# Moving VectorE's and ScalarE's side work, a check's small matmuls and the last block's transfers in a TensorE-bound two-layer kernel

## The chip, the cores and the metric

One core of one Trainium2 chip. The metric is the device time of a launch in microseconds (us), slowest core, median of runs; executions of one kernel mostly agree within 0.3%. A trace of one execution goes with it; its span is about 1.5 us shorter than the time.

## The reference

```python
batch, m, k, h, n = 16, 512, 768, 3072, 768        # x: (16, 512, 768)
y = np.maximum(np.matmul(x, w1) + b1, 0)
return np.matmul(y, w2).astype(np.float32)
```

## The kernel before

The 8192 rows are worked off in 16 blocks: 8 blocks of rows with the first half of the hidden units, then the same rows with the second half, whose results are added to the outputs that the first eight blocks wrote. Both products run in fp16 in a seven-product (Strassen-like) or 20-product form, so that TensorE does fewer matmuls and the other engines form sums of inputs, weights and results. The 20 products of the second layer are the 20 "steps" of a block; this table names what follows each (engine, where to, from which pair of PSUM banks):

```python
SECOND = (
    ("mm", 16, 1, True), ("mm", 4, 0, True), ("ACT", "s0", 1, 1), ...
    # ... steps 2 to 6
    ("mm", 11, 1, False),  ("DVE", "o2", 1, -1, "s4", 1),      # step 7: o2 = s4 - q1
    ("mm", 3, 0, False),   ("ACT", "s5", 0, 1),                # step 8
    ("mm", 8, 2, True),    ("ACT", "q1", 2, 1),                # step 9: banks q2 into banks q1
    ("mm", 1, 0, False),   ("DVE", "o3", 0, -1, "s0", 1),      # step 10
    ("mm", 13, 2, False),  ...                                 # step 11: adds into q2 again
    # ... steps 12 to 18
    ("mm", 7, 3, False),   ("DVE", "o6", 3, -1, "s4", 1),      # step 19
)
```

Steps and their products are counted from 0: in the texts below "product 11" is the product of step 11, written `("mm", 13, ...)`, which reads the weights' sum V13. V6, V14 and B5 are other blocks or sums of w2; the negated B5 is formed on ScalarE. VectorE's and ScalarE's work runs in the order in which the program emits it (the prediction shows it in a trace). Extra work (sums of weights and of x, squares for the range check, loads) is hooked behind a step by `put(kind, block, group, step, what)`; `"m1"` is a group of the first product, `"m2"` the second product:

```python
for n in range(15):                                   # sums of w2, two halves each, first block
    put("p1", 0, *divmod(min(10 + n // 2, 15), 4), self.sum_w2, n, 0, 2)
    late = {9: 1, 7: 2, 8: 3, 12: 4, 10: 5, 14: 6, 13: 7, 11: 8}.get(n)
    at = ("m2", 0, 0, late) if late else ("p1", 0, 4 + (n + 2) // 8, (n + 2) % 8 // 2)
    put(*at, self.sum_w2, n, 2, 4)
# ...
put("m2", it, 0, 1 + 4 * half + s, self.square_x, nxt, half, s)      # ScalarE
put("m2", it, 0, 6, self.sums_x, nxt, 0)                             # VectorE
put("m2", it, 0, 7, self.sums_x, nxt, 1)
# ...
put("m1", NSB + 3 + stage, 5, 6, self.out_of_range, stage)   # small fp32 matmuls into PSUM bank 4
```

In the second eight blocks an output goes out by an accumulating transfer from GpSimd, except five outputs of the last block, which are fetched early, added on GpSimd and written plainly:

```python
LAST = {"o7": ("s1", -1, 3), "o4": ("s5", 1, 15), "o1": ("s3", -1, 12), "o6": ("s4", 1, 16),
        "o5": ("s2", 1, 5)}
# ... in total():
if it < self.NSB or (final and to in self.LAST):
    (nc.scalar if final and to == "o1" else nc.sync).dma_start(out=rows, in_=o)
else:
    nc.gpsimd.dma_start(out=rows, in_=o, accum_op=ALU.add)
```

At the very end the program branches to a slow general path if the inputs were out of range (here they are in range):

```python
with tc.If(s.bad > 0, preferred_fallthrough_block=False):
    # ...
    general_path(general, tc, xf, w1, b1, w2, of)
```

## Time and profile before

| | before |
|---|---|
| time, median (range) | 878.19 us (878.11 to 878.46) |
| span of the trace | 876.6 us |
| TensorE busy | 865.9 us, 99% |
| shortest block of the steady part | 53.19 us |
| longest blocks of it | 53.90, 53.63, 53.59 us |
| from the last block's start to the end | 60.06 us |

How to read it: with TensorE at 99%, shares say no more. What matters is which blocks are longer than the floor that the matmuls alone need, and which link of which queue TensorE waited for there. The prediction shows those lines.

### The profile page before, as it was taken

How to read it: one execution, taken by the hardware profiler on the slowest of the kernel's cores; microseconds unless marked ns; L12 is line 12 of the kernel's file. 1: busy time of each engine (PE TensorE's matmuls, PEld its weight loads, DVE VectorE, ACT ScalarE, POOL GpSimd, SP SyncE). 2: the span in 40 equal slices, each digit the busy share in tenths (PEclk: the TensorE clock that was granted, in tenths of full speed). 3: DMA queues.
4: the chain of work that ended last, by engine and by line, in shares of the span. 5: the costliest groups of instructions: out<-in, count | busy, mean ns of one | idle time of the engine just before them, and what ended most of it. 6: DMA issues, size and time to landing. Idle time of an engine off the chain costs nothing.

```text
span 876.6 us, 12584 instructions
## 1 busy us (share of the span) xinstructions
PE 865.9 (99%) x4675; PEld 458.6 (52%) x4675; DVE 619.5 (71%) x1082; ACT 520.0 (59%) x792; POOL 194.8 (22%) x174
## 2 busy tenths in 40 slices
PE   9999999999999999999999999999999999999996
PEld 6454554545545454554545545455454555545453
DVE  3898767767686667866799676665866668566684
ACT  5765757768576775766356576775626345362541
POOL 7310240503305041040200402203030130401314
PEclk9999999999999999999999999999999999999999
DMA  9999698796978959549541836549264483726706
GB/s 206 198 229 270 122 260 204 142 256 151 281 157 197 249 93 272 119 183 341 219 180 55 131 98 167 91 132 138 76 128 68 146 125 120 104 47 163 108 19 147
DMA packets 121717, 140.08 MB, mean 160 GB/s; under 512 B 67228, under 2 KB 115124, under 8 KB 117812
## 3 DMA queue, kind: packets, MB, share of 16 engines
q0 software_dynamic: 49328, 44.44, 35.8%
q1 hardware_dynamic: 71584, 93.40, 32.6%
q10 hardware_dynamic: 740, 1.39, 0.4%
q8 instruction: 38, 0.62, 0.3%
q14 instruction: 27, 0.22, 0.1%
HBM read 74.13 MB, written 77.66 MB: 173 GB/s over the span
## 4 chain that ended last, share of the span: by engine, by line
PE 90%; DVE 5%; DMA 2%; POOL 1%; issue 1%; ACT 1%; DVEq 0%; POOLq 0%; ACTq 0%
PE ps L539 46%; PE ps L637 44%; DVE y L471 2%; DVE v L338 2%; DMA xn<-in_x_dram 1%; DMA v<-in_w_dram 1%; POOL w1s L277 1%; DVE o L682 0%; DVE s L682 0%; DVE y L551 0%; POOL s L622 0%; ACT ps L676 0%; DVE ps L682 0%; ACT s L547 0%; ACT y L556 0%
## 5 line engine op out<-in xcount | busy, mean ns | idle before, releaser
L637 PE MATMUL ps<-v,y 128*128 128x384 f16 x2560 | 424.3, 326 | 1.4 <-ACT ps L676 1.1
L539 PE MATMUL ps<-x,w1s 128*128 128x512 f16 x1890 | 415.6, 379 | 0.0
L637 PEld LDWEIGHTS <-y 128*128 128x128 f16 x2560 | 249.6, 98 | 173.0 <-ACT y L556 2.5
L539 PEld LDWEIGHTS <-w1s 128*128 128x128 f16 x1890 | 184.9, 98 | 218.5 <-issue 0.9
L547 ACT ACTIVATE s<-ps,b1y 128x512 f32<-128x512 f32 x210 | 142.2, 687 | 149.6 <-PE ps L539 69.2
L471 DVE TENSOR_TENSOR y<-y 128x512 f16<-128x512 f16 x512 | 203.4, 423 | 33.9 <-ACT y L556 25.4
L551 DVE CUSTOM_DVE_ANT_0 y<-ps,s 128x512 f16<-128x512 f32 x210 | 144.9, 690 | 102.6 <-PE ps L539 71.4
L676 ACT ACTIVATE s<-ps 128x768 f32<-128x768 f32 x96 | 77.7, 810 | 116.7 <-PE ps L637 95.2
L689 POOL DMA_DIRECT2D out_dram<-o x57 | 70.0, 1366 | 321.2 <-DVE o L682 321.2
L682 DVE TENSOR_TENSOR s<-ps,s 128x768 f32<-128x768 f32 x96 | 90.2, 953 | 12.0 <-PE ps L637 5.8
L556 ACT ACTIVATE y<-ps,b1y 128x512 f16<-128x512 f32 x90 | 61.9, 687 | 39.7 <-PE ps L539 39.7
L682 DVE TENSOR_TENSOR o<-s,ps 128x768 f32<-128x768 f32 x54 | 51.4, 951 | 47.9 <-PE ps L637 25.6
L682 DVE TENSOR_TENSOR o<-ps,s 128x768 f32<-128x768 f32 x54 | 50.4, 953 | 36.0 <-ACT s L676 35.4
L397 POOL TENSOR_TENSOR x<-x 128x3072 f16<-128x3072 f16 x7 | 42.0, 6007 | 65.2 <-DVE x L394 52.8
L277 POOL DMA_DIRECT2D x<-in_w_dram x12 | 10.1, 848 | 182.8 <-DMA xd<-x 88.2
L385 ACT ACTIVATE scrap<-xn 128x768 f16<-128x768 f16 x60 | 50.3, 838 | 0.8
L562 ACT ACTIVATE ps<-ps,b1y 128x512 f32<-128x512 f32 x60 | 39.6, 659 | 10.3 <-PE ps L539 7.5
L556 ACT ACTIVATE y<-ps 128x512 f16<-128x512 f32 x60 | 35.9, 598 | 0.0
L346 ACT ACTIVATE scrap<-scrap 128x1536 f16<-128x1536 f16 x24 | 35.4, 1476 | 0.1
L676 ACT ACTIVATE ps<-ps 128x768 f32<-128x768 f32 x32 | 25.5, 797 | 10.5 <-PE ps L637 8.4
L489 PE MATMUL ps<-x,w1s 128*128 128x512 f16 x132 | 29.0, 379 | 0.3 <-DVE x L444 0.3
L372 POOL DMA_DIRECT2D xn<-in_x_dram x16 | 12.1, 760 | 62.1 <-ACT scrap L385 61.8
(70 smaller groups left out, 293.2 us busy)
## 6 DMA issues: line engine op xcount, KB each, us to landing
out_dram<-o POOLq DMA_DIRECT2D x57, 384.0 KB, 6.0
out_dram<-o SPq DMA_DIRECT2D x51, 384.0 KB, 4.2
xd<-x SPq DMA_DIRECT2D x8, 1536.0 KB, 5.6
x<-xd SPq DMA_DIRECT2D x8, 1536.0 KB, 8.2
xn<-in_x_dram POOLq DMA_DIRECT2D x14, 768.0 KB, 7.2
xd<-x SPq DMA_DIRECT2D x7, 1152.0 KB, 8.5
x<-xd SPq DMA_DIRECT2D x7, 1152.0 KB, 5.2
out_dram<-x SPq DMA_DIRECT2D x16, 384.0 KB, 5.8
```

Of the source, the lines that this page charges most:

```text
L385: self.nc.scalar.activation(out=self.junk(self.K), in_=rows, func=ACTF.Square, accum_out=self.stat[:, i:i + 1])
L397: (self.nc.gpsimd if it > 1 else self.nc.vector).tensor_tensor(out=x[:, a21:self.XS2 + 1:self.XS2 - a21], in0=x[:, a21:self.XS1 + 1:self.X ...
L471: self.nc.vector.tensor_tensor(out=pair(*outs), in0=pair(*ins0), in1=pair(*ins1), op=ALU.add if sign > 0 else ALU.subtract)
L539: nc.tensor.matmul(ps, lhsT=w[:, slot, k, :], rhs=x[:, xslot, k, :], start=(start and k == 0), stop=(k == 2), skip_group_check=True)
L547: nc.scalar.activation(out=kept(name), in_=ps, func=ACTF.Identity, bias=bias)
L551: nc.vector._custom_dve(TENSOR_ADD_SAT, out=self.y_of(self.TP * half + t, m), in0=self.two(ps), in1=self.two(kept(name)), s0=F_MAX, s1=0.0)
L556: nc.scalar.activation(out=self.y_of(self.TP * half + t, m), in_=self.two(ps), func=ACTF.Relu, **kw)
L562: nc.scalar.activation(out=g["b"], in_=g["a"], func=ACTF.Identity, bias=bias1)
L637: nc.tensor.matmul(self.ps[:, 2 * q + j, 0:NH], lhsT=self.y[:, U_OF[p], m0:m0 + P], rhs=self.v[:, V_OF[p], s, :], start=(start and s == 0) ...
L676: nc.scalar.activation(out=o, in_=ps, func=ACTF.Copy, scale=float(sign))
L682: nc.vector.tensor_tensor(out=o, in0=a, in1=b, op=ALU.add if sign == kept_sign else ALU.subtract)
L689: nc.gpsimd.dma_start(out=rows, in_=o, accum_op=ALU.add)
```

## The change

Its intent: no accumulating transfer in the last block; squares placed where ScalarE has no sum to form; sums of weights spread over more steps of the two blocks in which they are made (the first and the ninth); and the range check's small matmuls moved by one group.

```diff
     LAST = {..., 
-            "o5": ("s2", 1, 5)}
+            "o5": ("s2", 1, 5), "o2": None, "o3": None, "o0": None}
@@ total()
+                if final and self.LAST[to] is None:
+                    self.add_last(to, o)                      # GpSimd adds the fetched rows
-                if it < self.NSB or (final and to in self.LAST):
-                    (nc.scalar if final and to == "o1" else nc.sync).dma_start(out=rows, in_=o)
+                if it < self.NSB or final:
+                    queue = nc.scalar if final and to == "o1" else nc.sync
+                    kept_back.append(lambda: queue.dma_start(out=rows, in_=o))
+                    if not final or to != "o0":               # o0 goes out behind o5
+                        while kept_back:
+                            kept_back.pop()()
@@ plan()
-            late = {9: 1, 7: 2, 8: 3, 12: 4, 10: 5, 14: 6, 13: 7, 11: 8}.get(n)
+            late = {9: 1, 7: 2, 8: 3, 12: 8, 10: 9, 14: 10, 11: 11, 13: 12}.get(n)
-        put("m2", 0, 0, 12, self.sum_w2, 15)
+        put("m2", 0, 0, 13, self.sum_w2, 15)
-                        put("m2", it, 0, 1 + 4 * half + s, self.square_x, nxt, half, s)
+                        put("m2", it, 0, (3, 4, 4, 7, 9, 10, 10, 12)[4 * half + s], self.square_x, ...)
-                put("m2", it, 0, 6, self.sums_x, nxt, 0)
-                put("m2", it, 0, 7, self.sums_x, nxt, 1)
+                put("m2", it, 0, 6 if it else 7, self.sums_x, nxt, 0)
+                put("m2", it, 0, 7 if it else 9, self.sums_x, nxt, 1)
-                      (10, ("m2", NSB, 0, 5)), (14, ("m2", NSB, 0, 6)),        # ninth block
-                      (13, ("m2", NSB, 0, 9)), (11, ("m2", NSB, 0, 12))):
+                      (10, ("m2", NSB, 0, 8)), (14, ("m2", NSB, 0, 10)),
+                      (13, ("m2", NSB, 0, 11)), (11, ("m2", NSB, 0, 12))):
-            put("m1", NSB + 3 + stage, 5, 6, self.out_of_range, stage)
+            put("m1", NSB + 3 + stage, 4, 6, self.out_of_range, stage)
# cut: the x loads that follow their squares, the weights' squares (stat_w1), one sum of w1,
# the order of the fetches of the last block's old rows, and add_last's new argument o
```

More of the change, by code (lines that the diff above doesn't have):

```diff
@@ L616, in fetch_last, with add_last @@
         self.nc.sync.dma_start(out=self.x_outputs(slot), in_=self.rows_of(self.NIT - 1, to))
-    def add_last(self, to):
+    def add_last(self, to, o=None):
         slot = list(self.LAST).index(to)
-        name, sign, _ = self.LAST[to]
-        s = self.s[:, int(name[1])].rearrange("p (a n) -> p a n", a=2)
+        s, sign = o, 1
+        if o is None:
+            name, sign, _ = self.LAST[to]
+            s = self.s[:, int(name[1])].rearrange("p (a n) -> p a n", a=2)
         self.nc.gpsimd.tensor_tensor(out=s, in0=s, in1=self.x_outputs(slot),
@@ L646, in at @@
             return self.s[:, int(name[1])].rearrange("p (a n) -> p a n", a=2)
-        pairs = {}
+        pairs, kept_back = {}, []
         def output(to):
@@ L819, in plan @@
             put("p1", 0, *at, lambda t: self.sums_w1(self.w1s[t], vector, (0, 1, 2)), t)
-            put(*(("m1", 1, t - 1, 2) if t else ("m2", 0, 0, 10)),
+            put(*(("m1", 1, t - 1, 2) if t else ("m2", 0, 0, 13)),
                 lambda t: self.sums_w1(self.w1s[t], vector, (3,)), t)
@@ L837, in plan @@
                     for s in range(4):
-                        put("m2", it, 0, 1 + 4 * half + s, self.square_x, nxt, half, s)
+                        put("m2", it, 0, (3, 4, 4, 7, 9, 10, 10, 12)[4 * half + s],
+                            self.square_x, nxt, half, s)
                 if nxt + 1 < NSB:
-                    put("m2", it, 0, 5, self.load_x, nxt + 1, (0,))
-                    put("m2", it, 0, 9, self.load_x, nxt + 1, (1,))
+                    put("m2", it, 0, 7, self.load_x, nxt + 1, (0,))
+                    put("m2", it, 0, 12, self.load_x, nxt + 1, (1,))
                 put("m1", nxt, 1, 0, self.save_x, nxt, 1)
@@ L871, in plan @@
                       (4, ("m1", NSB, 1, 3)), (5, ("m1", NSB, 2, 1)), (12, ("m1", NSB, 2, 3)),
-                      (10, ("m2", NSB, 0, 5)), (14, ("m2", NSB, 0, 6)),
-                      (13, ("m2", NSB, 0, 9)), (11, ("m2", NSB, 0, 12))):
+                      (10, ("m2", NSB, 0, 8)), (14, ("m2", NSB, 0, 10)),
+                      (13, ("m2", NSB, 0, 11)), (11, ("m2", NSB, 0, 12))):
             put(*at, self.sum_w2, n)
-        for to, (_, _, i) in self.LAST.items():
-            put(*(("m2", NIT - 1, 0, 1) if to == "o5" else ("m1", NIT - 1, 1, 6)),
-                self.fetch_last, to)
-            put("m2", NIT - 1, 0, i, self.add_last, to)
+        for n, (to, what) in enumerate(self.LAST.items()):
+            put(*(("m1", NIT - 1, 1, 6) if n < 4 else ("m2", NIT - 1, 0, 1)), self.fetch_last, to)
+            if what is not None:
+                put("m2", NIT - 1, 0, what[2], self.add_last, to)
         for t in range(TP):
             for n in range(3):
-                put("m2", 1 + t, 0, 11 + 3 * n, self.stat_w1, 0, t, n)
-                put("m2", NSB + t // 2, 0, 3 + 9 * (t % 2) + 2 * n, self.stat_w1, 1, t, n)
+                put("m2", 1 + t, 0, (13, 15, 17)[n], self.stat_w1, 0, t, n)
+                put("m2", NSB + t // 2, 0, ((3, 9, 10), (12, 15, 17))[t % 2][n], self.stat_w1, 1,
+                    t, n)
         for n in range(8):
```

## The prediction

> **What bounds the kernel now.** I read the page first, for which engine is busy, and then cut the span at the block boundaries with the view of stretches, because a share over the whole span cannot show where a busy engine still loses time.
>
> ```profile
> PE 865.9 (99%) x4675; PEld 458.6 (52%) x4675; DVE 619.5 (71%) x1082; ACT 520.0 (59%) x792; POOL 194.8 (22%) x174
> ...
> PE 90%; DVE 5%; DMA 2%; POOL 1%; issue 1%; ACT 1%; DVEq 0%; POOLq 0%; ACTq 0%
> ```
>
> TensorE (PE) is busy 99% of 876.6 us and is 90% of the chain that ended last, at a granted clock of 1.00. The change removes no large matmul, so it can only win where PE waits. Stretches from one block to the next (columns: start:end, length, PE, weight loads, VectorE, ScalarE, GpSimd, clock, DMA):
>
> ```profile
> 0.00:69.91 69.91, 67.38 (x385) 39.73 (x386) 50.95 (x104) 42.71 (x75) 26.32 (x48) 1.00 1.22 214
> ...
> 389.44:442.64 53.20, 53.20 (x287) 27.92 (x286) 38.64 (x66) 26.14 (x37) 6.00 (x1) 1.00 0.79 291
> 442.64:496.54 53.90, 53.49 (x287) 27.88 (x286) 47.31 (x77) 32.60 (x44) 7.01 (x7) 1.00 0.40 99
> ...
> 602.93:656.56 53.63, 53.50 (x289) 28.22 (x288) 36.85 (x67) 24.66 (x36) 9.73 (x10) 1.00 0.54 112
> 656.56:710.15 53.59, 53.48 (x289) 28.22 (x288) 35.98 (x63) 24.66 (x36) 9.75 (x10) 1.00 0.53 110
> ...
> 816.54:876.60 60.06, 52.55 (x284) 27.41 (x281) 38.29 (x64) 24.78 (x36) 15.66 (x11) 0.98 0.45 88
> ```
>
> The floor of a block comes from two rows of the chain in order of time: 117 matmuls of the first product in 25.25 us (0.2158 each) and 144 of the second in 23.43 us (0.1627 each). A block has 126 and 160: 27.19 + 26.03 = 53.22 us. Eleven of the blocks stand within 0.1 us of it. The rest are few: the first block, the one at 442.64 (53.90), the two at 602.93 and 656.56 (53.63, 53.59), and the end. What PE waits for, in the view of waits, is almost nothing else:
>
> ```profile
> PE ps L637 <- ACT ps L676: 1.1, 2, 0.7
> ```
>
> Two waits, 0.74 and 0.41 us. Back along the chain, the first looks like this:
>
> ```profile
> 53.72 1.01 DVE v L338 x2
> 54.73 0.87 DVE x L394
> 55.60 0.88 DVE o L682
> 56.50 0.02 ACTq L676
> 56.56 0.80 ACT ps L676
> 57.41 4.71 PE ps L637 x28
> ```
>
> Product 11 of the block adds into banks that ScalarE empties into another bank pair (ACT ps), which it may not overwrite until VectorE has taken output o2 out of it (DVE o). That o2 is late because VectorE is first doing weights' sums (v) and x sums. The same three links carry the second wait: o2 at 482.23, ACT at 483.19, PE at 484.03.
>
> **What the Trainium skill says.** "PSUM — Partial Sum Buffer", section "Engine vs sequencer instructions": the queues of ScalarE, VectorE and GpSimd are strict FIFO, and matmuls start and complete in program order. The chain above agrees: o2 begins at 55.52, when the x sum is done, though PE had finished its product near 52.7. "DMA: Bandwidth & Descriptors", section "SWDGE vs HWDGE vs iDMA": accumulating in a transfer is to be had only from GpSimd's software queue. The trace agrees: accumulating outputs stand on POOL, 1.2 us of GpSimd per issue in the last block. The same page, section "Issuing engines are not separate DMA queues": transfers of all issuers interleave on the same 16 engines. The end agrees in that all queues share one full set, shown below. "SBUF — State Buffer", section "SBUF: two separate sides": VectorE with two SBUF inputs and a GpSimd operation reading SBUF lock each other out. I see no case of it where it counts: GpSimd's adds last 1.81 to 2.14 us, and the sums out of PSUM beside them keep 0.95 us.
>
> **The change, part by part.**
>
> (1) Weights' sums and x sums, first block. Before o2 (step 7 of 20) stood half sums after steps 1 to 6; three of them (V13, V6, V14) and the first x sum move behind it. That frees VectorE of 3 x 0.47 + 0.87 = 2.3 us ahead of o2 (rows of the chain). PE should have gone on at 42.21 + 11 x 1.30 = 56.52; it started at 57.41. Gain 0.89 us: the visible wait of 0.74 and 0.15 of refilling the pipeline. Does the queue behind o2 now block something? With T7 the end of step 7: o2 until T7 + 1.45, x sum 2.3, two half sums 3.3, the large x sum (1.67 net) 4.95, o3 5.85. Product 13 needs o3 gone at T7 + 6.5. It fits with 0.6 us to spare; the next sum fits with about the same. On ScalarE the negated B5 (1.48 us), one step later now, is ready about 0.2 us before step 16 needs it: the tightest place.
>
> (2) The same for the block at 442.64: sums 10 and 14 (0.87 each) leave the place ahead of o2 (1.82 us at 480.41, the pair just before it). Gain 0.41 + 0.15 = 0.56 us. Its other 0.14 us lies in the first product and stays.
>
> (3) The range check's two small matmuls go one first-product group earlier. Now they stand between the second product's first and second step, and step 2 writes PSUM bank 4, which the check also uses: its loads stand idle 0.36 us until VectorE has copied the sums out (the copy ends at 632.29, PE goes on at 632.35). In the new place bank 4 is not wanted for some 8 us. Of 0.43 and 0.39 us over the floor, about 0.14 each is the matmul itself and stays: gain 0.29 + 0.25 = 0.54 us. The 1.3 us of tiny VectorE work now falls among the first product's sums, where it has idle pieces of 0.6 to 0.9 us and PE about 1.2 us of slack per bank.
>
> (4) Squares: 60 of 0.84 + 0.19 us move between ScalarE's sums. The blocks with them are already at 53.2, so this pays nothing there. Fit: three squares (3.1 us) after step 3 until step 6 (3.9 us), three after step 9 until step 12. Gain 0. The weights' squares (1.48 each): the one after step 12 can make the sum of step 13 0.2 us late; its bank is wanted only 1.3 us after that, so nothing.
>
> (5) The end. Three accumulating transfers of 384 KB become three early fetches, three GpSimd adds and three plain transfers. GpSimd: an add costs 1.9 us against 1.2 us of issue, 0.7 us more each, and o3's and o0's stand in a busy stretch. The last GpSimd add (before: 867.13 to 868.94) is what the last VectorE subtraction (868.96) waited for; with an add of o0 at 863.2 ahead of two others it should start 0.1 to 0.3 us later. But that is not what ends the span. The same view of stretches, half microseconds of the tail:
>
> ```profile
> 865.00:865.50 0.50, 0.50 (x5) 0.29 (x3) 0.50 (x2) 0.00 (x0) 0.50 (x1) 1.00 1.08 52
> ...
> 867.00:867.50 0.50, 0.50 (x5) 0.31 (x4) 0.48 (x1) 0.00 (x0) 0.38 (x1) 1.00 1.17 206
> ...
> 869.00:869.50 0.50, 0.09 (x1) 0.00 (x0) 0.50 (x2) 0.00 (x0) 0.00 (x0) 1.00 1.05 375
> ...
> 872.50:873.00 0.50, 0.00 (x0) 0.00 (x0) 0.00 (x0) 0.00 (x0) 0.00 (x0) 1.00 0.94 332
> ```
>
> The 16 engines are full from 865 to 873.5 us: until 868 with the accumulating o0 at 52 to 230 GB/s, then with plain outputs at about 360. Making o0 plain frees roughly 2 us of engine time (3 us down to 393 KB / 360 GB/s = 1.1). But o5, then o0, will be through by about 868.5, and o7 is only computed at 868.0. The four outputs from o7 on are 1.57 MB, 4.4 us, from about 868.9 on: again 873.3. So I expect o0's 2 us mostly to turn into idle engines before 868.9. I book 0.2 us of gain for the end, and 0.2 us of loss for small new waits anywhere.
>
> **The sum.** 0.89 + 0.56 + 0.54 = 1.99 us, plus 0, gives 878.19 - 2.0 = 876.2 us; I say 876.1.
>
> **Rivals.** First: the tail pays more. If the accumulating transfer also holds back o5 and o7 by more than I think, or slows the straggling last packets (a few still run at 874 to 875.5 us with the engines nearly idle), the end comes 0.5 to 1 us earlier: about 875.3. For it: o5, issued at 865.27, shows no packet until after 867.5. Against: bytes from o7 on alone fill 4.4 us. Second: GpSimd becomes the tail's bound. Its adds of o3 (from 858.5), s3, o0, s5, s4 leave it about 1 us of air in total; if each runs to 2.14 us, s4's add and the last subtraction slip 0.5 us or more, and the time is about 876.7. Third: VectorE's queue is late again further down in the first block (o3, or the q2 sum after it) and takes 0.3 to 0.7 us back: also about 876.7. Fourth: the check's small operations stall the first products of two blocks: at most 0.5 us lost. None is near 2% (17.6 us), since everything but PE's floor and the fixed head and end is under 3 us.
>
> **Range and chances.** The sure part is 2 us; the rivals spread it from 0.7 to 3.2 us: 875.0 to 877.4. Within 2% is as good as certain.
>
> **What would show it.** Right: PE's waits on ACT ps gone from the view of waits; stretches of the four blocks 0.89, 0.56, 0.29, 0.25 us shorter; other blocks still 53.2; from the end of the last product to the end of the span unchanged within 0.4 us, with the engines idle before about 866.5. Wrong: a new PE wait of over 0.3 us on DVE o or ACT v in the first block; the two check blocks still at 53.6; an end that moves by more than 0.6 us either way.

## The result, and the profile after

| | before | after |
|---|---|---|
| time, median (range), 6 runs each | 878.19 us (878.11 to 878.46) | 875.91 us (875.86 to 876.16) |
| span of the trace | 876.6 us | 874.5 us |
| from the start of the first second product to the end of the first block | 27.70 us | 26.81 us |
| ninth block | 53.90 us | 53.33 us |
| the two blocks with the check's matmuls | 53.63, 53.59 us | 53.34, 53.33 us |
| from the last block's start to the end | 60.06 us | 60.15 us |

The ratio is 0.9974 (95% interval 0.9961 to 0.9987): clear of 1. Ratios here are the mean time of one kernel's runs over that of the other's of the same rounds, so not quite the ratio of the medians quoted. The interval is about 1.1 us wide to each side. So tenths of a microsecond can't be read from the times; they are read from the traces, one each, whose steady blocks repeat within 0.1 us.

The line of busy times on the page after (each engine's busy us, share of the span, instructions):

```profile
PE 864.4 (99%) x4675; PEld 457.4 (52%) x4675; DVE 619.6 (71%) x1082; ACT 523.7 (60%) x792; POOL 196.6 (22%) x174
```

TensorE does the same 4675 matmuls, and its share stays 99%: a share does not show this change. Its whole list in the view of waits after:

```profile
PE ps L360 <- DVE ones L238: 1.3, 1, 1.3
PE ps L438 <- DMA o<-in_x_dram: 0.6, 2, 0.3
PE ps L489 <- DVE x L444: 0.3, 1, 0.3
PE ps L438 <- DMA xn<-in_x_dram: 0.2, 1, 0.2
```

The two waits on `ACT ps` are gone, and what is left are waits of the first 19 us, before any steady work. The stretches between block ends of the changed kernel:

```profile
0.00:68.95 68.95, 66.48 (x385) 38.56 (x386) 50.79 (x104) 43.06 (x75) 26.26 (x48) 1.00 1.21 213
...
441.57:494.90 53.33, 53.33 (x287) 27.89 (x286) 47.32 (x77) 32.71 (x44) 7.00 (x7) 1.00 0.41 101
...
601.29:654.63 53.34, 53.34 (x290) 28.17 (x288) 36.94 (x67) 24.69 (x36) 9.73 (x10) 1.00 0.53 112
654.63:707.96 53.33, 53.33 (x289) 28.17 (x288) 36.11 (x63) 24.69 (x36) 9.75 (x10) 1.00 0.53 111
...
814.35:874.50 60.15, 52.55 (x283) 27.45 (x281) 38.29 (x64) 24.77 (x36) 17.34 (x11) 0.97 0.41 108
```

In every steady block PE's busy time is now the whole length of the block. Of the 2.10 us of span, the first block gives 0.89, its head 0.07 (42.21 to 42.14 until the first second product), the ninth block 0.57, the two check blocks 0.29 and 0.26, the other blocks together 0.11; the last stretch gives back 0.09.

This is the link that was late, now on time, in the order of time of the changed kernel (start, length, engine, line, operation; in brackets the idle time before it and what ended that):

```profile
53.36 0.94 DVE L684 TENSOR_TENSOR o<-s,ps 128x768 f32<-128x768 f32 x1
...
54.22 0.95 DVE L394 TENSOR_TENSOR x<-x 128x1536 f16<-128x1536 f16 x1
...
55.34 0.80 ACT L678 ACTIVATE ps<-ps 128x768 f32<-128x768 f32 x1 [0.49 <-PE ps L639]
```

Output o2 starts at 53.36 instead of 55.52, ahead of the x sum; ScalarE's copy waits for the matmul (PE), no longer for VectorE. The copy starts at 55.34, and o2 had ended at 54.30: o2 has 1.0 us to spare.

### The profile page after: what moved, and what is told of

Same layout as the page of the kernel before. It is cut to its first block, busy times and chain, and to the rows that moved or that the text cites. A ratio compares the mean times of both kernels' runs of the same rounds, so it can differ in the third digit from the quotient of the medians.

```text
span 874.5 us, 12597 instructions
## 1 busy us (share of the span) xinstructions
PE 864.4 (99%) x4675; PEld 457.4 (52%) x4675; DVE 619.6 (71%) x1082; ACT 523.7 (60%) x792; POOL 196.6 (22%) x174
## 4 chain that ended last, share of the span: by engine, by line
PE 96%; DMA 1%; POOL 1%; DVE 1%; issue 0%; ACT 0%; DVEq 0%; POOLq 0%
PE ps L639 47%; PE ps L539 47%; PE ps L489 3%; DMA xn<-in_x_dram 1%; POOL w1s L277 1%; DVE ps L684 0%; POOL s L624 0%; DVE o L684 0%; PE ps L438 0%; ACT s L678 0%; DVE o L672 0%; DVE x L444 0%; POOL ident masks.py:199 0%; POOL ident L229 0%; POOL high L244 0%
## 5 line engine op out<-in xcount | busy, mean ns | idle before, releaser
L697 POOL DMA_DIRECT2D out_dram<-o x54 | 66.4, 1375 | 315.9 <-DVE o L684 315.9
```

## The experiments

Twelve kernels ran, each the changed kernel with one part (or a set of parts) put back or taken out; all are correct unless said. "First stretch" is the time from the first matmul of the first second product to the end of the first block: 26.81 us after, 27.70 us before. It leaves out the head, which varies from trace to trace with the first transfers (the first second product starts between 41.84 and 42.57 us).

| run | time, median (range) | ratio to before | reading from its trace |
|---|---|---|---|
| sums of the first block back (u_sums0) | 877.83 (877.71 to 878.13) | 0.9995 | first stretch 28.36 |
| sums of the ninth block back (u_sums8) | 876.72 (876.58 to 876.94) | 0.9982 | ninth block 53.92 |
| check's matmuls back (u_check) | 876.70 (876.63 to 876.93) | 0.9981 | blocks 53.62, 53.60 |
| accumulating transfers back (u_last) | 875.91 (875.73 to 876.41) | 0.9972 | last stretch 60.02 |
| squares back (u_squares) | 876.36 (876.14 to 876.47) | 0.9977 | first stretch 26.81 |
| sums and squares back (u_sums0_sq) | 877.58 (877.12 to 877.77) | 0.9985 | first stretch 28.45 |
| only the x sums moved (x_only) | 877.07 (877.00 to 877.14) | 0.9985 | first stretch 27.93 |
| only V13 moved (one_half) | 878.02 (877.93 to 878.25) | 0.9996 | first stretch 28.74 |
| only the small x sum back (x0_ahead) | 876.00 (875.90 to 876.16) | 0.9969 | first stretch 26.80 |
| one last output left out (drop_o7) | 875.84 (875.83 to 876.49) | 0.9974 | last stretch 59.90 |
| no general path (no_general) | 874.94 (874.80 to 875.00) | 0.9957 | last stretch 58.32 |
| other layout of the branch (fall_true) | 875.22 (874.91 to 876.23) | 0.9961 | last stretch 60.45 |

### The ninth block, and the check

```diff
-                      (10, ("m2", NSB, 0, 8)), (14, ("m2", NSB, 0, 10)),
-                      (13, ("m2", NSB, 0, 11)), (11, ("m2", NSB, 0, 12))):
+                      (10, ("m2", NSB, 0, 5)), (14, ("m2", NSB, 0, 6)),
+                      (13, ("m2", NSB, 0, 9)), (11, ("m2", NSB, 0, 12))):
```

> The changed kernel with the weights' sums of the ninth block (the one that began at 441.57 us) put back. Theory: that block grows from 53.33 to 53.89 us, PE waits 0.41 us on ACT ps there, span about 875.06, time about 876.5 us. Rival (this block was long for another reason, such as the w2 reads of raw tiles or the weights' squares): below 53.5 us, span within 0.2 of 874.5.

The wait is back, in the view of waits of this run, and the block is 53.92 us, 0.59 longer:

```profile
PE ps L639 <- ACT ps L678: 0.4, 1, 0.4
```

The theory holds; the rival is out, since the weights' squares stayed moved and did not matter.

```diff
-            put("m1", NSB + 3 + stage, 4, 6, self.out_of_range, stage)
+            put("m1", NSB + 3 + stage, 5, 6, self.out_of_range, stage)
```

> The changed kernel with the range check's two small matmuls put back between the second product's first two steps. Theory (PSUM bank 4 is wanted by step 2 before VectorE has emptied it): the two blocks grow from 53.34 and 53.33 to 53.63 and 53.59 us, span about 875.05, time about 876.4 us. Rival (the fp32 matmuls and their weight loads themselves cost it, wherever they stand): below 53.45 us each, span within 0.2 of 874.5.

The blocks are 53.62 and 53.60 us against 53.34 and 53.33: 0.28 and 0.27 us. The chain of this run shows what TensorE waited for in the first of them:

```profile
630.00 0.75 DVE y L471 x2
630.75 0.11 DVE stat L730
630.86 0.04 issue
630.90 3.25 PE ps L639 x19
```

The copy of the check's sums out of bank 4 (`stat`) stands behind other VectorE work, and the matmuls into bank 4 start when it is done. The rival is only the remainder: with the wait gone the blocks still stand 0.13 us over the neighbours' 53.19 to 53.20, which is the small matmul itself.

### The first block

```diff
-            late = {9: 1, 7: 2, 8: 3, 12: 8, 10: 9, 14: 10, 11: 11, 13: 12}.get(n)
+            late = {9: 1, 7: 2, 8: 3, 12: 4, 10: 5, 14: 6, 13: 7, 11: 8}.get(n)
-                put("m2", it, 0, 6 if it else 7, self.sums_x, nxt, 0)
-                put("m2", it, 0, 7 if it else 9, self.sums_x, nxt, 1)
+                put("m2", it, 0, 6, self.sums_x, nxt, 0)
+                put("m2", it, 0, 7, self.sums_x, nxt, 1)
# and the negated B5 back to step 12, one sum of w1 back to step 10
```

> The changed kernel with the first block's sums (weights' sums and x sums) put back where they were; the squares stay moved. Theory (VectorE's queue ahead of output o2 made PE wait): PE's wait on ACT ps of about 0.74 us is back near 57.3 us, the first stretch (to the end of the block) grows from 68.95 to about 69.84 us, the span from 874.5 to 875.4, the time to about 876.8 us; the other blocks unchanged. Rival (ScalarE was late because of the squares ahead of its sum, and moving the squares is what cured it): no wait or less than 0.3 us, span below 874.8.

More than expected came back: 1.55 us in the first stretch, not 0.89. There are two waits now:

```profile
PE ps L639 <- ACT ps L678: 0.9, 1, 0.9
...
PE ps L639 <- ACT s L678: 0.3, 1, 0.3
```

With 0.15 us of refilling after each, 0.93 + 0.31 + 0.30 = 1.54 us. The first is the wait before, somewhat longer. The second is new. After ScalarE's late copy, three squares, the negation of B5 and a fourth square stood ahead of its next sum (`s`), which ran from 62.31 to 63.1, while the product that adds into the same banks was due at 62.8. So in this trace the squares' new places fit only with sums that are on time. The other side of that:

```diff
-                        put("m2", it, 0, (3, 4, 4, 7, 9, 10, 10, 12)[4 * half + s], self.square_x, ...)
+                        put("m2", it, 0, 1 + 4 * half + s, self.square_x, nxt, half, s)
# likewise the x loads and the weights' squares
```

> The changed kernel with the squares of x and of the weights (and the loads that follow them) put back where they were; all sums stay moved. Theory (squares cost nothing where they stood): span within 0.15 us of 874.5, every block within 0.05 of the changed kernel's; at most 0.15 us in the first block, where a square after step 8 ends 0.4 us after ScalarE could empty the banks for product 11. Rival (the squares carry part of the first block's gain): 0.3 us or more in the first stretch, a PE wait on ACT ps.

With the squares in their old places and the sums moved, the first stretch is 26.81 us, as after, and TensorE has no such wait. From the end of the first block to the start of the last it takes 745.57 us against 745.40: 0.17 us for all squares. The times differ by 0.45 us, within what the heads (42.37 against 42.14 us in the traces) and the intervals allow. In this trace the squares carry no part of the first block's gain.

Putting both back should then give the kernel before in this block:

```diff
# both edits above
```

> The changed kernel with both the first block's sums and all squares put back (the check, the ninth block's sums and the last block stay changed). Theory (the sums alone make the 0.89 us of the first block; that putting back the sums alone cost 1.55 us in that stretch is because squares in the new places stand ahead of ScalarE's sum when PE's product 11 comes late): the stretch from the first second-product matmul to the end of the block is 27.70 us as in the kernel before, PE waits 0.74 on ACT ps and nothing on ACT s. Rival (the extra 0.66 us has another cause): 28.3 us again.

It did not: 28.45 us, with a single wait of 1.46 us. The chain of this run names a cause that no earlier trace had shown:

```profile
50.05 5.17 DMA x<-xn
55.22 0.03 issue
...
55.34 0.09 DVE x L394
...
56.22 0.96 DVE o L684
...
57.26 0.80 ACT ps L678
```

The small x sum (`x`) needs the last of eight transposing transfers, which landed at 55.22 us here. VectorE stood idle for it for 0.26 us, and o2 behind it began at 56.22 instead of 55.52. So my expectation fell, and by its number the rival came true, although the mechanism (o2 late in the queue) stood: the sum ahead of o2 also ties o2 to a transfer that is not always in time. With the squares in their old places there is no wait on `ACT s`, though product 11 came later than in u_sums0. Up to the end of the first block this run is the same program as the kernel before, so 27.70 and 28.45 us are two executions of one program. No undoing gave 27.70 back: the 0.89 us is what one pair of traces shows, and in other executions the gain can be larger. This run's five times spread over 0.65 us, and those of the kernel before over 1.04 us in the same rounds (878.05 to 879.09; 0.35 to 0.54 in the other rounds), against 0.30 us for the changed kernel. That the same transfer makes the spread is likely but not shown; only one trace caught it. A rival stays untested too: the next x load is hooked behind the squares, so here it is issued at 50.72 us, and GpSimd's software queue takes 54% of the 16 engines from 52 to 54 us, while the last transposes are on their way. In the changed kernel and in u_sums0 it is issued at 53.36 and 53.31, and that queue moves nothing from 48 to 56. In the kernel before and in u_squares it is issued as early (50.75 and 50.91), yet the transposes were in time there. No run moves the load alone.

```diff
-                put("m2", it, 0, 6 if it else 7, self.sums_x, nxt, 0)
+                put("m2", it, 0, 6, self.sums_x, nxt, 0)
```

> The changed kernel with one thing put back: the first block's small x sum stands ahead of output o2 again, all other sums stay behind it. The profile of the last undoing showed this sum waiting for the transposed x (landed 55.22 us) and o2 waiting behind it in VectorE's queue, although its other profile-mates found the data landed by about 53. Theory (o2's place in the queue counts, and 0.87 us is within the 1.0 us of slack that o2 has in the changed kernel): where the transposes are in time, no PE wait, first second-product stretch 26.81 us, time about 875.9 us; where they land late, o2 is late with them, PE waits on ACT ps, and the runs spread by up to 1 us upward. Rival (the x sum always waits there for its transposes): every run about 1 us slower, PE wait on ACT ps of 0.5 us or more in the profile.

In the changed kernel the small x sum may stand ahead of o2: first stretch 26.80 us, no TensorE wait, o2 at 54.24 and done 0.1 us before ScalarE's copy at 55.28. The transposes were in time in the traced run and the six times spread over 0.26 us, so the late landing was not met again; but this run keeps the x load at its later place (53.29 us), so it does not test what made it late. This fits the 1.0 us of slack. It also says that of the 2.3 us taken from ahead of o2 the weights' sums alone would have done (here the large x sum stays moved too, behind o2 in both cases). Would the x sums alone?

```diff
# the changed kernel with the weights' sums (late = ...) put back, the x sums moved
```

> The changed kernel, but in the first block only the two x sums stay moved, the weights' sums are put back. Theory (o2's delay is the sum of what stands ahead of it in VectorE's queue): o2 is 0.87 us earlier than with all put back, PE gets back 0.87 of 0.89 us: wait on ACT ps gone or at most 0.1 us, first stretch 68.95 to 69.1. Rival (the x sum could not begin earlier because it waits for its transposes, and the queue is not what counts): the wait stays near 0.7.

No. The old wait on `ACT ps` is no longer listed, and only a rest of it is left: product 11 starts at 56.71 us, right behind ScalarE's copy (ended at 56.67), 0.27 us after its turn at 56.44. But a new one stands a little later, in the view of waits:

```profile
PE ps L639 <- DVE o L684: 0.7, 1, 0.7
```

In order of time (ScalarE's copy, the large x sum, output o3):

```profile
55.87 0.80 ACT L678 ACTIVATE ps<-ps 128x768 f32<-128x768 f32 x1 [1.01 <-DVE o L684]
...
57.50 1.75 DVE L397 TENSOR_TENSOR x<-x 128x3072 f16<-128x3072 f16 x1
...
59.17 0.94 DVE L684 TENSOR_TENSOR o<-s,ps 128x768 f32<-128x768 f32 x1
```

The large x sum, now after step 9, began at 57.50 us behind the weights' sums and ran until 59.2; output o3 came behind it, and product 13 needs o3's banks. Of the 1.12 us over the changed kernel this wait and its refill are 0.84, the rest of the old one 0.27. So the expected stretch (at most 0.15 us longer) was missed: most of what was gained at o2 was paid at o3.

```diff
# the changed kernel with all first-block sums put back, but V13 after step 8
```

> The changed kernel, but in the first block only one half sum of the weights (V13, 0.47 us) stays moved from step 4 to step 8; the rest put back. Theory (dose): PE's wait shrinks from 0.74 to about 0.27 us, first stretch about 69.37 us, span about 874.95. Rival (a threshold or another link sets it): 0.74 or 0.

The dose itself came out: the wait on `ACT ps` is 0.23 us, of an expected 0.27. But a larger one was made:

```profile
PE ps L639 <- DVE v L338: 1.4, 1, 1.4
...
PE ps L639 <- ACT ps L678: 0.2, 1, 0.2
```

V13 itself is the moving operand of product 11. After step 8 it stood behind the large x sum, which was still hooked to step 7, and came 1.38 us late. The first stretch is 28.74 us, worse than before. So the change's first part works as a whole: the half sums may move back only because the large x sum moves behind them.

### The tail

```diff
-            "o5": ("s2", 1, 5), "o2": None, "o3": None, "o0": None}
+            "o5": ("s2", 1, 5)}
# and the accumulating transfers for o2, o3, o0 as before
```

> The changed kernel with the three accumulating transfers of the last block put back. Theory (the tail is set by the four outputs that are ready from 865.8 us on, whatever came before): the last stretch stays within 0.2 us of 60.15, more likely 60.06 as before, span 874.3 to 874.6, time 875.6 to 876.1 us, though the DMA engines are full from about 863 us on again. Rival (the accumulating transfer holds back the plain ones): last stretch 60.6 or more, span 875 or more.

The last stretch is 60.02 us, the time 875.91 us as after: this part of the change is worth nothing that can be measured. (The span of the trace, 874.8, is longer because its head is: the first second product starts at 42.57 instead of 42.14.) The theory's outcome is right. Was its reason? It said that the bytes of the four last outputs fill the end.

```diff
-                if it < self.NSB or final:
+                if final and to == "o7":
+                    pass
+                elif it < self.NSB or final:
```

> Wrong on purpose: the changed kernel without the last block's transfer of output o7 (384 KB, 1.1 us at 360 GB/s); its rows keep what an earlier block wrote. Theory (the end is set by the bytes of the four outputs that come last): the bulk of transfers ends about 1.1 us earlier, span 873.3 to 873.9. Rival (the end is set by one straggling engine's last packets, or by latency from the last VectorE subtraction at 867.8 us): span within 0.4 of 874.5.

Its output is wrong, which doesn't matter for the time. With 1.1 us of transfers fewer, the last stretch is only 0.25 us shorter, and the last two half outputs, issued at 867.4 and 867.9, still take 5.2 us to land (5.5 before, after and in u_last). The reason that I gave is wrong: a gap opened among the transfers instead, from about 866.3 to 867.5 us, and the rest came no earlier. (That o7's bytes do not count does not say that those of the last three outputs don't; no run takes them away.) What is it then? In the trace after, the bulk of transfers is over by 871.2 us, and this is the queue view from 871 to 873.5 (packets, MB, share of the 16 engines):

```profile
q1 hardware_dynamic: 49, 0.06, 14.1%
q8 instruction: 1, 0.02, 2.9%
q14 instruction: 2, 0.02, 2.1%
q10 hardware_dynamic: 14, 0.02, 2.0%
```

Some 60 packets of outputs trickle in over 2 us with instruction fetches among them. "Runtime: NRT & Kernel Launch" of the Trainium skill, section "Instruction fetch mechanics", says that each sequencer fetches 16 KiB blocks of instructions over a DMA queue of its own, and that a taken branch whose target is outside its window has to fetch the target first. The trace agrees in that instruction packets run on queues of their own (q8, q14), one of 16 KB; the program ends with a branch, but whether its target lies outside the window no run shows.

```diff
-    with tc.If(s.bad > 0, preferred_fallthrough_block=False):
-        with ExitStack() as general:
-            general_path(general, tc, xf, w1, b1, w2, of)
```

> The changed kernel without the general path and the branch to it at the end (correct for these inputs, which are in range). In the tail one straggling share of the last outputs lands 1.8 us after the bulk of them, while instructions are fetched over the same 16 engines. Theory (the fetch for the branch at the end holds one engine up): no instruction fetch near 871 us, transfers end with the bulk at about 871.3, span about 872.7 to 873.3, time about 1.5 us less. Rival (the straggler is there whatever is fetched, or latency sets the end): span within 0.4 of 874.5.

The last stretch falls by 1.83 us to 58.32, the last halves land 3.6 us after their issue instead of 5.5, and from 871 us to the end no packet moves at all:

```profile
814.08:872.40 58.32, 52.55 (x284) 27.46 (x281) 38.28 (x64) 24.78 (x36) 17.34 (x11) 0.97 0.41 110
```

The time falls less than the span, to 874.94 us, about 1.0 below the changed kernel. The intervals of the two ratios overlap (0.9943 to 0.9970 against 0.9961 to 0.9987), but the times do not: 874.80 to 875.00 against 875.86 to 876.16, and 875.90 to 876.16 for x0_ahead, which ran on the same chip. The traced execution took 874.87 us with a span of 872.4, 2.5 us apart, the changed kernel's 876.13 with 874.5, 1.6 us apart; why is not settled. So the conditional path at the end holds up the end of the span by 1.8 us; that the fetching is how fits the page and the packets, but this edit also takes out the branch itself, so the two are not told apart. The kernel without the general path is no proposal: it gives up the inputs that are out of range.

```diff
-    with tc.If(s.bad > 0, preferred_fallthrough_block=False):
+    with tc.If(s.bad > 0, preferred_fallthrough_block=True):
```

> The changed kernel with the general path laid out as the preferred fall-through of the branch at the end. If the fetch of instructions at the end sets the last microseconds, the layout changes them: a different span by 0.3 us or more, either way. If it does not, span 874.5 within 0.3.

Inconclusive. The five times fall in two groups, 874.91 to 875.22 and 876.13 to 876.23; the traced run is of the second, with a last stretch of 60.45 us. The spans follow: 873.4, 873.5 and 873.7 us in the first group, outside the 874.5 within 0.3 of the expectation, 874.6 and 874.7 in the second, inside it. Why an execution falls in one or the other no trace shows. The median, 875.22, is 0.7 us under the changed kernel's, but the intervals overlap (0.9948 to 0.9975 against 0.9961 to 0.9987), so I don't call it a version that beats both.

## Why the prediction was right, point by point

- **TensorE bounds, and only its waits can be won.** Right: all matmuls stayed, and the span fell by what the waits were.
- **(1) First block, 0.89 us.** Right in size: 27.70 to 26.81. The cause is the place of the sums ahead of o2: with them back the stretch is 28.36 or 28.45 (u_sums0, u_sums0_sq), with only the squares back it stays 26.81 (u_squares). That the size came out to the hundredth is in part luck, since the undoings gave 1.55 and 1.64. Two things were missing. The x sum ahead of o2 also waits for transposing transfers that may be late (55.22 us in u_sums0_sq). And the slack was counted for the whole change only; parts of it would have lost it elsewhere (x_only, one_half). My 0.6 us of slack for o3 was 0.4: it ends at 58.64, product 13 starts at about 59.05. The negated B5 ended at 62.72, 0.2 us ahead of its product, as worked out.
- **(2) Ninth block, 0.56 us.** Right: 0.57, and 0.59 when undone.
- **(3) Check, 0.29 + 0.25 us.** Right: 0.29 and 0.26; the small matmul's own 0.14 stayed.
- **(4) Squares, 0.** Right in the traces, with 0.17 us at most; whether the x load that moved with them keeps the transposes in time is open. Not foreseen: in their new places they make ScalarE less forgiving when a sum comes late.
- **(5) The end, 0.** Right in size (0.09 us longer), wrong in its reason. The engines did stand idle until 863.9, as foreseen, and o0's saving did vanish there. But the end did not follow from 4.4 us of bytes from o7 on: without o7's 1.1 us it came 0.25 us earlier (drop_o7), without the conditional path 1.83 us (no_general). That this error did not show in the number is luck: the old transfers and the new ones end alike (u_last: 60.02 us). GpSimd's last add did not slip by 0.1 to 0.3 us either: it began 50.57 us into the block, before 50.59. From o2's on the adds took 1.80 to 1.82 us each, instead of up to 2.14.
- **The sum.** 1.99 us predicted in the parts, 2.01 measured in them; the 2.28 us between the medians has the head and the other blocks as well (0.07 and 0.11), and the traced execution after took 876.13 us, 0.22 over its median. No rival came true in the change itself. The third did in two of its parts alone.

## What to carry to other kernels

When one engine is busy 99% of the time, compare equal blocks with the floor of that engine, and go back from each excess along the chain to the first instruction that stood in a queue ahead of a needed one; here 2.0 of the span's 2.1 us were found this way before the run. Moving work behind the needed instruction pays only if the next deadlines in that queue have room: count them all, and move a set whole, because half of it can cost more than none. Where a tail is argued from bytes, take bytes away and look whether the end moves.

## What the Trainium skill lacked or had wrong

- "Runtime: NRT & Kernel Launch", section "Instruction fetch mechanics", names the stall of the branching engine, not what a conditional block at the end does to others: here the last half outputs landed 5.5 us after issue with it and 3.6 us without, and the last stretch was 1.83 us shorter without.
- "DMA: Bandwidth & Descriptors", section "SWDGE vs HWDGE vs iDMA", says who may accumulate in a transfer, not what that costs a kernel's own output: one 384 KB accumulating output held 94% of the 16 engines from 864.9 to 868.1 us of the trace before (about 3.0 us of all of them), where a plain one moves at about 360 GB/s (1.1 us). No run tells the adding from GpSimd's queue.
- No page that I found says that VectorE's strict order can tie an unrelated output to a transfer: in one trace a sum waiting for a transpose held o2 back, and TensorE waited 1.46 us instead of 0.74. "PSUM — Partial Sum Buffer", section "Engine vs sequencer instructions", has the rule (strict FIFO) without that consequence.
